# The first norm of a two-layer encoder: one product with a tile of ones and 1/sqrt on ScalarE, with thirteen unread products behind it

## The chip, the cores and the metric

The kernel runs on one core of a Trainium2 chip. The metric is the device time of one execution in microseconds (us). Before the change the median of three runs is 2392.25 us (2389.51 to 2394.10).

## The reference

Two layers run over one sequence of 512 tokens (T) with 1024 channels (D). Each layer has three sub-layers: a feed-forward part (SwiGLU, 2816 wide), a mixer, a second feed-forward part. Each of them begins in the same way, and only this beginning is touched, and only for the first sub-layer of the first layer:

```python
def rms_norm(x, gain):
    y = xf * lax.rsqrt(jnp.mean(xf * xf, axis=-1, keepdims=True) + EPS)
    return (y * gain)
def modulate(h, shift, scale):
    return h * (1 + scale[:, None, :]) + shift[:, None, :]
...
    c_act = jax.nn.silu(c)
    mod = (c_act @ w_ada[l] + b_ada[l]).reshape(B, N_MOD, D_MODEL)
    h = modulate(rms_norm(x, norm_gain[l, 0]), mod[:, 0], mod[:, 1])
    x = x + 0.5 * mod[:, 2][:, None, :] * swiglu(h, ...)
```

Each token needs the reciprocal root of the mean square of its 1024 channels, and each channel a shift and a scale, which are dot products of 1024 numbers of silu(c) with a row of w_ada.

## The kernel before, in words

The activations lie transposed: channels on the 128 partitions, tokens along the row. Eight slices d of 128 channels (KD = 8) make up D. All products are done in three parts to keep precision: a number is split into a high part (hi) and a rest (lo), and the function `triple` (L119, L120, L121) adds hi·hi, lo·hi and hi·lo into one accumulator. For the first norm the names are `hhi` and `hlo` for the two parts of the normalized x, and `whi` and `wlo` for those of the weights.

The opening is written out in `start()`:

1. While x arrives in four blocks, ScalarE squares it (L150), and VectorE adds the eight squared tiles into `ssum` (L693, L695): 128 partitions with 512 tokens each, still to be summed over the partitions.
2. Four small products with a column of ones (L699) sum over the partitions and leave the tokens on the partitions, four columns of 128. There VectorE works out 1/sqrt with the integer estimate and three Newton steps of three instructions (L299, L306 to L308). Since the result is needed along the row, for all partitions alike, it is spread over four diagonal tiles (L708 on ScalarE, L710 on VectorE), and one product with a tile of ones (L713) puts it into the accumulator `rb`, 128x512.
3. Eight steps d follow. In each, `h(d)` computes t = rb·x on VectorE (L722), hhi on ScalarE (L724), a copy of the same value `tb` in PSUM (L726), and hlo = tb − hhi on VectorE (L727). `product(d)` then issues 18 matmuls: for six accumulators (three columns of the gate matrix and three of the up matrix) one each of L119, L120 and L121.

What feeds the steps is loaded by SyncE in program order: per step one weight chunk w_first (384 KB, two buffers `raw`) and two rows of w_ada (512 KB each, four buffers `v2`), one for the shift (j = 0) and one for the scale (j = 1) of the next slice. A buffer is loaded again when its reader is done. Each row of w_ada is turned into 128 shifts or scales by one dot product on VectorE (`mod_dot`, L206; its result tile is `modc`, and its big output goes back into the loaded tile, which the trace calls `v`). ScalarE makes the factor `apre` out of a scale (L213), and hhi(d) needs it. Each weight chunk is rounded to `whi` by ScalarE (L290), and GpSimd computes `wlo` = raw − whi (L292). After the eight steps the same accumulators are evacuated (L571 is the Silu), and the next unit's weights follow in the same way, with wlo on VectorE.

The order on each engine is decided by a scheduler. `tc.issue_after(x)` and `behind(engine)` only tell it that an instruction is to stand behind another one in its engine's queue. So the engines' queues are shown below where they differ.

Of the kernel before, what the change touches and what calls it, by code (L numbers as in the profile page):

```python
# [40 lines left out]
def encoder_kernel(tc, xT, c, w_ada, b_ada, gains, w_gate, w_up, w_down, w_qkv, w_f, w_ubg,  # L41
# [93 lines left out]
    make_identity(nc, ident)  # L135
    ones = cp.tile([P, P], F32, name="ones")
    nc.vector.memset(ones, 1.0)
    silc = [st([P, D], F32, "b", NB)]
    sil_dram = dr.tile([1, D], F32, name="sil_dram")
    crow = st([1, D], F32, "b", NB)  # L140
# [62 lines left out]
    def mod_dot(raw, l, j, d):  # L203
        m = modc[:, l, j, d:d + 1]
        with after("norm"):
            dot = nc.vector.tensor_tensor_reduce(out=raw, in0=raw, in1=silc[0], scale=1.0,  # L206
                                                 scalar=badac[:, l, j, d:d + 1], op0=ALU.mult, op1=ALU.add,
                                                 accum_out=m).ins
        s, kind = divmod(j, 3)
        if kind == 1:  # L210
            g = gainc[:, l, s, d:d + 1]
            if in_start[0]:
                nc.scalar.activation(apre[:, l, s, d:d + 1], m, AF.Identity, scale=g, bias=g)  # L213
                return dot
            return nc.vector.scalar_tensor_tensor(apre[:, l, s, d:d + 1], m, 1.0, g, op0=ALU.add, op1=ALU.mult).ins
        if kind == 2:
            nc.vector.tensor_scalar(m, m, 0.5, None, op0=ALU.mult)

    mod_queue = [(l, j, d) for l in range(L) for j in range(9) for d in range(KD)][16:]
    mod_ptr = [0]  # L220
# [354 lines left out]
    class Ffn:  # L575
# [112 lines left out]
        def start(self):  # L688

            l = self.l  # L690
            ssum = st([P, T], F32, "ssum", 1)
            tiles = [sq[:, a, :] for sq in squares for a in range(2)]
            fold = nc.vector.tensor_tensor(ssum, tiles[0], tiles[1], op=ALU.add)  # L693
            for tile_ in tiles[2:]:
                fold = nc.vector.tensor_tensor(ssum, ssum, tile_, op=ALU.add)  # L695
            gate["vector"] = fold.ins
            pv = mmt((P, NT))
            for t in range(NT):
                mm(pv[:, t:t + 1], ssum[:, t * P:(t + 1) * P], ones[:, 0:1], start=True, stop=True)  # L699
            with behind("vector"):  # L700
                mod_step(l, 0, 0, "v2")
            v = st([P, NT], F32, "nt_v4", 1)
            nc.vector.tensor_scalar(v, pv, 1.0 / D, EPS, op0=ALU.mult, op1=ALU.add)
            r = rsqrt(v, NT)
            dg = st([P, NT, P], F32, "ssum", 1)
            for t in range(NT):
                if t % 2:
                    nc.scalar.activation(dg[:, t, :], ident, AF.Copy, scale=r[:, t:t + 1])  # L708
                else:
                    gate["vector"] = nc.vector.tensor_scalar(dg[:, t, :], ident, r[:, t:t + 1], None, op0=ALU.mult).ins  # L710
            spread = gate["vector"]
            rb = mmt()
            mm(rb, ones, dg.rearrange("p a b -> p (a b)"), start=True, stop=True)  # L713
            pgs = [(acc(), acc()), (acc(), acc()), (mmt(), mmt())]

            with behind("vector"):
                ready = [mod_step(l, 1, 0, "v2")]
            gate.clear()

            def h(d):  # L720
                t = t1(T)
                scaled = nc.vector.tensor_tensor(t, rb, xd(d), op=ALU.mult).ins  # L722
                a, b = apre[:, l, 0, d:d + 1], modc[:, l, 0, d:d + 1]
                nc.scalar.activation(hhi[:, d, :], t, AF.Identity, scale=a, bias=b)  # L724
                tb = mmt()
                nc.scalar.activation(tb, t, AF.Identity, scale=a, bias=b)  # L726
                nc.vector.tensor_tensor(hlo[:, d, :], tb, hhi[:, d, :].bitcast(F32), op=ALU.subtract)  # L727
                if d + 1 < KD:
                    with tc.issue_after(ready[0]):
                        mod_step(l, 0, d + 1, "v2")  # L730
                    with tc.issue_after(scaled):
                        ready[0] = mod_step(l, 1, d + 1, "v2")

            def product(d, w):
                for n in range(3):
                    for which in range(2):
                        i = 3 * which + n
                        triple(pgs[n][which], w[0][:, i, :], w[1][:, i, :], hhi[:, d, :], hlo[:, d, :],
                               d == 0, d == KD - 1)

            for d in range(KD):
                if d == 0:
                    gate["vector"] = spread
                w = wchunk(w_first[d], (6, P), side=False, lo_eng=nc.gpsimd)
                gate.clear()
                h(d)
                product(d, w)
            in_start[0] = False
            self.early = self.gate_up(0, 3), self.gate_up(1, 3)
            late_inputs()  # L750
            return [self.act(n, *pgs[n]) for n in range(3)]
# [557 lines left out]
```

## Time and profile before

| what | value |
|---|---|
| median of three runs | 2392.25 us |
| the profiled execution's own time | 2394.31 us |
| its span in the trace | 2392.4 us |
| TensorE busy in the span | 2357.9 us (99%) |
| VectorE busy in the span | 1738.8 us (73%) |
| first matmul of step d = 0 (L119) | 21.81 us |
| first matmul behind the eight steps | 59.09 us |

The profiled execution is 2.1 us above the median of the runs and inside their spread (its upper end is 2394.10) but for 0.2 us. Of its own time 1.9 us lie outside the span. Times in rows count from the span's start. A row of the timeline gives start, length, engine, line, operation, output and inputs, and in brackets how long the engine stood idle before it and what ended that. PE is TensorE, DVE is VectorE, ACT is ScalarE, POOL is GpSimd, SP is SyncE.

### The profile page before, as it was taken

To read this page: it belongs to the slowest core of one execution; us is meant where nothing else is said; L and a number is where in the kernel's file an instruction comes from. 1 tells how busy PE (TensorE), PEld (TensorE's weight loads), DVE (VectorE), ACT (ScalarE), POOL (GpSimd) and SP (SyncE) were. 2 spreads that over 40 slices of the span, in tenths; PEclk is the share of its full clock that TensorE was granted. 3 is DMA by queue.
4 is the path that set the end of the run, shared out by engine and by line. 5 is a ranking of instruction groups with operands and counts; after the bars stand their busy time and mean duration, and the time that the engine had idled before them with its cause. 6 is when DMAs were issued, how large, how long until landed. Compare 5 with 4: busy or idle time off the path is not lost.

```text
span 2392.4 us, 36842 instructions
## 1 busy us (share of the span) xinstructions
PE 2357.9 (99%) x14106; PEld 2086.4 (87%) x14106; DVE 1738.8 (73%) x3090; ACT 1201.4 (50%) x2090; POOL 315.9 (13%) x401
## 2 busy tenths in 40 slices
PE   7999999999999999999999999999999999999999
PEld 5898998778888898989998989978788888889898
DVE  8887866787685576878677878577866855768583
ACT  5353555786632353635553636466865324536252
POOL 3000011144312200000000000102443222000000
PEclk9999999999999999999999999999999999999999
DMA  7535342223355534353325353323233554223322
GB/s 284 203 106 185 105 143 80 94 80 109 119 199 200 193 106 151 115 178 105 133 80 194 101 190 106 135 84 100 78 117 111 220 202 158 99 96 106 104 96 102
DMA packets 116436, 320.93 MB, mean 134 GB/s; under 512 B 11138, under 2 KB 13314, under 8 KB 116260
## 3 DMA queue, kind: packets, MB, share of 16 engines
q1 hardware_dynamic: 115106, 314.38, 38.6%
q0 software_dynamic: 1152, 4.19, 0.4%
q8 instruction: 111, 1.82, 0.3%
q14 instruction: 65, 0.53, 0.1%
q10 hardware_dynamic: 2, 0.00, 0.0%
HBM read 312.16 MB, written 6.38 MB: 133 GB/s over the span
## 4 chain that ended last, share of the span: by engine, by line
PE 85%; DVE 7%; ACT 5%; issue 2%; DMA 1%; SPq 0%; DVEq 0%; ACTq 0%; POOL 0%; POOLq 0%
PE acc L119 15%; PE acc L120 15%; PE acc L121 15%; PE mm L119 4%; PE mm L120 4%; PE mm L121 4%; PE mm L129 4%; PE mm L128 4%; PE mm L130 4%; PE acc L128 4%; PE acc L129 4%; PE acc L130 4%; ACT b L859 1%; PE mm L997 1%; DVE v L206 1%
## 5 line engine op out<-in xcount | busy, mean ns | idle before, releaser
L290 ACT CAST whi<-raw 128x1024 fp32r<-128x1024 f32 (+1 forms) x267 | 277.4, 1043 | 438.3 <-PE acc L120 255.7
L292 DVE TENSOR_TENSOR wlo<-raw,whi 128x1024 fp32r<-128x1024 f32 x259 | 319.6, 1237 | 160.5 <-ACT whi L290 157.8
L119 PE MATMUL acc<-b,whi 128*128 128x512 f32 (+1 forms) x960 | 360.7, 376 | 0.0
L120 PE MATMUL acc<-b,whi 128*128 128x512 f32 (+1 forms) x960 | 357.0, 372 | 0.0
L121 PE MATMUL acc<-b,wlo 128*128 128x512 f32 (+1 forms) x960 | 356.6, 371 | 0.0
L119 PEld LDWEIGHTS acc<-b,whi 128*128 128x128 f32 x960 | 180.8, 188 | 31.7 <-DVE xv L447 0.3
L121 PEld LDWEIGHTS acc<-b,wlo 128*128 128x128 f32 x960 | 180.8, 188 | 31.5
L120 PEld LDWEIGHTS acc<-b,whi 128*128 128x128 f32 x960 | 180.9, 188 | 29.8
L119 PE MATMUL acc<-hhi,whi 128*128 128x512 f32 x480 | 191.1, 399 | 3.3 <-ACT hhi L724 1.7
L120 PE MATMUL acc<-hlo,whi 128*128 128x512 f32 x480 | 188.3, 392 | 1.4 <-DVE hlo L727 1.4
L121 PE MATMUL acc<-hhi,wlo 128*128 128x512 f32 x480 | 188.0, 392 | 0.0
L398 DVE TENSOR_TENSOR ptb<-v,ptb 128x1024 fp32r<-128x1024 f32 x128 | 156.6, 1224 | 35.8 <-ACT ptb L397 33.9
L397 ACT CAST ptb<-v 128x1024 fp32r<-128x1024 f32 x128 | 134.0, 1050 | 95.4 <-DVE v L465 54.6
L397 ACT CAST whi<-raw 128x1024 fp32r<-128x1024 f32 (+1 forms) x128 | 106.7, 834 | 99.2 <-PE acc L120 52.8
L119 PE MATMUL acc<-whi,hhi 128*128 128x512 f32 x336 | 137.8, 411 | 0.9 <-DVE xv L398 0.9
L121 PE MATMUL acc<-whi,hlo 128*128 128x512 f32 x336 | 131.9, 393 | 0.0
L120 PE MATMUL acc<-wlo,hhi 128*128 128x512 f32 x336 | 131.7, 392 | 0.0
L206 DVE CUSTOM_DVE_ANT_0 v<-v,b,badac 128x1024 f32<-128x1024 f32 x87 | 116.1, 1341 | 20.5 <-DMA v<-in_w_ada_dram 20.3
L398 DVE TENSOR_TENSOR wlo<-raw,whi 128x1024 fp32r<-128x1024 f32 (+1 forms) x128 | 122.0, 953 | 6.8 <-ACT whi L397 5.0
L447 DVE SCALAR_TENSOR_TENSOR xv<-acc,modc,xv 128x512 f32<-128x512 f32 (+1 forms) x112 | 77.3, 691 | 63.4 <-PE acc L121 63.4
L119 PEld LDWEIGHTS acc<-hhi,whi 128*128 128x128 f32 x480 | 90.7, 189 | 21.4 <-ACT hhi L724 3.3
L119 PE MATMUL mm<-hhi,whi 128*128 128x512 f32 x280 | 109.3, 391 | 0.0
(313 smaller groups left out, 6594.9 us busy)
## 6 DMA issues: line engine op xcount, KB each, us to landing
raw<-in_w_down_dram SPq DMA_DIRECT2D x88, 512.0 KB, 3.7
v<-in_w_ada_dram SPq DMA_DIRECT2D x87, 512.0 KB, 5.4
raw<-in_w_up_dram SPq DMA_DIRECT2D x82, 512.0 KB, 3.9
raw<-in_w_gate_dram SPq DMA_DIRECT2D x79, 512.0 KB, 3.6
b<-in_w_ada_dram SPq DMA_DIRECT2D x57, 512.0 KB, 5.2
raw<-in_w_ubg_dram SPq DMA_DIRECT2D x56, 512.0 KB, 3.5
raw<-in_w_qkv_dram SPq DMA_DIRECT2D x42, 512.0 KB, 3.6
raw<-in_w_branch_dram SPq DMA_DIRECT2D x24, 512.0 KB, 3.6
```

The costliest lines, as they stand in the source:

```text
L119: mm(o, lh, rh, start=start, stop=False)
L120: mm(o, lh, rl, start=False, stop=False)
L121: mm(o, ll, rh, start=False, stop=stop)
L128: mm(o, lh, rh, start=start and k == 0, stop=False, skip_group_check=True)
L129: mm(o, lh, rl, start=False, stop=False, skip_group_check=True)
L130: mm(o, ll, rh, start=False, stop=k == 3, skip_group_check=True)
L206: dot = nc.vector.tensor_tensor_reduce(out=raw, in0=raw, in1=silc[0], scale=1.0, scalar=badac[:, l, j, d:d + 1], op0=ALU.mult, op1=ALU.add ...
L290: nc.scalar.copy(hi, raw)
L292: lo_eng.tensor_tensor(lo, raw, hi.bitcast(F32), op=ALU.subtract)
L397: nc.scalar.copy(hi, src)
L398: nc.vector.tensor_tensor(lo, src, hi.bitcast(F32), op=ALU.subtract)
L447: nc.vector.scalar_tensor_tensor(x, acc_j, gate, x, op0=ALU.mult, op1=ALU.add)
```

## The change

`ssum` is now multiplied once by the whole tile of ones, so that the sum over the partitions stands in all 128 partitions, tokens along the row (`total`, 128x512 in PSUM). The estimate of 1/sqrt is taken on ScalarE straight from there (`seed`), its square too, and VectorE does one Newton step on 128x512 elements with three instructions, of which the last writes `rb` into PSUM. The diagonal tiles and the nine small Newton instructions are gone. Behind the product stand thirteen products of two constant tiles, `ones` and `ident`, each 128x128, which nothing reads. The scale's dot product for d = 0 is asked for earlier, and inside a step the order asked for is now: t(d), shift dot of d+1, hlo(d), scale dot of d+1. The line `return dot` lets the shift's dot be named.

```diff
+    eps = cp.tile([P, 1], F32, name="eps")
+    nc.vector.memset(eps, EPS)
...
+        return dot
...
-            pv = mmt((P, NT))
-            for t in range(NT):
-                mm(pv[:, t:t + 1], ssum[:, t * P:(t + 1) * P], ones[:, 0:1], start=True, stop=True)
+            total = mmt()
+            mm(total, ones, ssum, start=True, stop=True)
+            spin = mmt((P, P))
+            for _ in range(13):
+                mm(spin, ones, ident, start=True, stop=True)
             with behind("vector"):
                 mod_step(l, 0, 0, "v2")
-            v = st([P, NT], F32, "nt_v4", 1)
-            nc.vector.tensor_scalar(v, pv, 1.0 / D, EPS, op0=ALU.mult, op1=ALU.add)
-            r = rsqrt(v, NT)
-            dg = st([P, NT, P], F32, "ssum", 1)
-            for t in range(NT):
-                if t % 2:
-                    nc.scalar.activation(dg[:, t, :], ident, AF.Copy, scale=r[:, t:t + 1])
-                else:
-                    gate["vector"] = nc.vector.tensor_scalar(dg[:, t, :], ident, r[:, t:t + 1], None, op0=ALU.mult).ins
-            spread = gate["vector"]
+                mod_step(l, 1, 0, "v2")
+            seed, square = t2(T), t2(T)
+            nc.scalar.activation(seed, total, AF.Abs_reciprocal_sqrt, scale=1.0 / D, bias=eps)
+            gate["scalar"] = nc.scalar.activation(square, seed, AF.Square).ins
+            var = t1(T)
+            nc.vector.tensor_scalar(var, total, 1.0 / D, EPS, op0=ALU.mult, op1=ALU.add)
             rb = mmt()
-            mm(rb, ones, dg.rearrange("p a b -> p (a b)"), start=True, stop=True)
+            nc.vector.scalar_tensor_tensor(var, square, -0.5, var, op0=ALU.mult, op1=ALU.mult)
+            nc.vector.scalar_tensor_tensor(rb, var, 1.5, seed, op0=ALU.add, op1=ALU.mult)
             pgs = [(acc(), acc()), (acc(), acc()), (mmt(), mmt())]
-
-            with behind("vector"):
-                ready = [mod_step(l, 1, 0, "v2")]
-            gate.clear()
...
-                nc.vector.tensor_tensor(hlo[:, d, :], tb, hhi[:, d, :].bitcast(F32), op=ALU.subtract)
-                if d + 1 < KD:
-                    with tc.issue_after(ready[0]):
-                        mod_step(l, 0, d + 1, "v2")
-                    with tc.issue_after(scaled):
-                        ready[0] = mod_step(l, 1, d + 1, "v2")
+                low = lambda: nc.vector.tensor_tensor(hlo[:, d, :], tb, hhi[:, d, :].bitcast(F32), op=ALU.subtract).ins
+                if d + 1 == KD:
+                    low()
+                    return
+                with tc.issue_after(scaled):
+                    shift = mod_step(l, 0, d + 1, "v2")
+                with tc.issue_after(shift):
+                    done = low()
+                with tc.issue_after(done):
+                    mod_step(l, 1, d + 1, "v2")
...
             for d in range(KD):
-                if d == 0:
-                    gate["vector"] = spread
                 w = wchunk(w_first[d], (6, P), side=False, lo_eng=nc.gpsimd)
```

Three places show how the queues move. The first is VectorE's queue in the opening norm, before the change, from the scale's dot product of slice 0 (`v_35`) back to the small Newton instructions ahead of it. `nt_v`, `nt_q`, `nt_u` and `nt_z` are the four-column tiles of the estimate; `t_39` is t of step 0.

```order
L307 SCALAR_TENSOR_TENSOR nt_u_153<-nt_q_152,nt_v_16_136 128x4
L308 SCALAR_TENSOR_TENSOR nt_z_154<-nt_u_153,nt_z_148 128x4
L710 TENSOR_SCALAR ssum_158<-ident,nt_z_154 128x128 x2
L206 ISA v_35_171,modc<-v_35_171,b_73,badac 128x1024
L206 ISA modc 128x1
L206 ISA v_41_187,modc<-v_41_187,b_73,badac 128x1024
L206 ISA modc 128x1
L722 TENSOR_TENSOR t_39_181<-mm_163,xv_78 128x512
```

This is the same place with the change. `v_17` is the scale's dot product of slice 0, `v_33` the shift's of slice 1, `t_20` is `var`, `t_19` and `t_18` are `square` and `seed`, and `mm_159` is `rb`.

```order
L208 ISA v_16_146,modc<-v_16_146,b_75,badac 128x1024
L208 ISA modc 128x1
L208 ISA v_17_149,modc<-v_17_149,b_75,badac 128x1024
L208 ISA modc 128x1
L712 TENSOR_SCALAR t_20_157<-mm_130 128x512
L714 SCALAR_TENSOR_TENSOR t_20_157<-t_19_154,t_20_157 128x512
L715 SCALAR_TENSOR_TENSOR mm_159<-t_20_157,t_18_153 128x512
L720 TENSOR_TENSOR t_31_174<-mm_159,xv_80 128x512
L208 ISA v_33_179,modc<-v_33_179,b_75,badac 128x1024
```

Eleven small instructions and two of 128x128 have given way to three of 128x512; both dot products of slice 0 stand ahead of them, and the first dot product of slice 1 has moved from ahead of t(0) to behind it.

The second place is VectorE's queue in the middle of the steps. With the change, from t of step 2 (`t_45`) to hlo of step 3 (out of `mm_288`); `v_41` and `v_48` are the scale's dots of slices 2 and 3, `v_47` is the shift's of slice 3.

```order
L720 TENSOR_TENSOR t_45_248<-mm_159,xv_87 128x512
L725 TENSOR_TENSOR hlo<-mm_214,hhi 128x512
L208 ISA v_41_220,modc<-v_41_220,b_75,badac 128x1024
L208 ISA modc 128x1
L208 ISA v_47_253,modc<-v_47_253,b_75,badac 128x1024
L208 ISA modc 128x1
L720 TENSOR_TENSOR t_52_285<-mm_159,xv_87 128x512
L725 TENSOR_TENSOR hlo<-mm_251,hhi 128x512
L208 ISA v_48_257,modc<-v_48_257,b_75,badac 128x1024
```

From step 0 to step 4 the order is now the same: t(d+1), hlo(d), scale dot of d+1, shift dot of d+2; from there on the shift dot stands between t and hlo. Before, the order changed from step to step, and both dots of a slice could run ahead of the hlo of the slice before it. TensorE's queue follows: of the 18 matmuls of a step, the ones that need only hhi (L119) stood one ahead of the first that needs hlo in steps 1 to 7; now there are 6, 5, 4, 3, 2, 1 and in step 7 again 6 of them ahead.

The third place is ScalarE's queue in the opening norm with the change; `t_18` is `seed`, `t_19` is `square`, `whi_170` the first weight chunk.

```order
L159 COPY b_75<-mm_92 128x512
L709 ACT_TABLE_LOAD
L709 ACTIVATE t_18_153<-mm_130,eps 128x512
L215 ACTIVATE apre<-modc,gainc 128x1
L710 ACTIVATE t_19_154<-t_18_153 128x512
L293 CAST whi_170<-raw_168 128x768
L722 ACTIVATE hhi<-t_31_174,modc,apre 128x512
L724 ACTIVATE mm_177<-t_31_174,modc,apre 128x512
```

A load of another function table stands ahead of the estimate (and a second one, back, ahead of the first Silu behind the steps); the first weight cast, which stood ahead of the norm's own work, now stands behind `square`.

## The prediction

> **What bounds the kernel now.** I read the busy times first, then what TensorE waited for in the first 60 us, then two windows, and then the timeline around the change.
>
> ```profile
> PE 2357.9 (99%) x14106; PEld 2086.4 (87%) x14106; DVE 1738.8 (73%) x3090; ACT 1201.4 (50%) x2090; POOL 315.9 (13%) x401
> ```
>
> ```profile
> PE mm L713 <- ACT ssum L708: 4.6, 1, 4.6
> PE mm L699 <- DVE ssum L695: 4.1, 1, 4.1
> PE acc L119 <- ACT hhi L724: 1.7, 1, 1.7
> PE acc L120 <- DVE hlo L727: 1.4, 2, 1.0
> ```
>
> ```profile
> 20.20:55.10 34.90, 31.88 (x128) 25.34 (x128) 34.73 (x46) 20.16 (x30) 15.73 (x7) 1.00 0.81 293
> 55.00:100.00 45.00, 44.91 (x198) 37.19 (x199) 43.98 (x67) 19.84 (x25) 0.00 (x0) 1.00 0.69 233
> ```
>
> Over the whole span TensorE is the bound: an opening that ends x us earlier should end the kernel x us earlier, since from 55 to 100 us TensorE idles for only 0.09 us. Inside the opening it looks otherwise. The columns of a window are its length and then the busy time of PE, PEld, DVE, ACT and POOL: during the eight steps VectorE is busy for 34.73 of 34.90 us, more than TensorE's 31.88. The opening hangs on VectorE's queue, and TensorE runs close behind it. The last step shows that:
>
> ```profile
> 53.67 0.39 PE L119 MATMUL acc<-hhi,whi 128*128 128x512 f32 x1
> 54.35 0.68 DVE L727 TENSOR_TENSOR hlo<-mm,hhi 128x512 fp32r<-128x512 f32 x1
> 55.09 0.50 PE L120 MATMUL acc<-hlo,whi 128*128 128x512 f32 x1 [1.04 <-DVE hlo L727]
> 59.09 0.39 PE L119 MATMUL mm<-hhi,whi 128*128 128x512 f32 x1
> ```
>
> The last hlo ends at 55.03, the 17 matmuls behind it take 4.00, and at 59.09 the eight steps are over. **The question is where this 59.09 goes.**
>
> **The opening norm, step by step.**
>
> ```profile
> 5.94 1.15 ACT L150 ACTIVATE wlo<-xv 128x512 f32<-128x512 f32 x2
> 10.17 1.05 ACT L157 COPY b<-mm 128x512 f32<-128x512 f32 x2
> 11.46 1.28 DVE L206 CUSTOM_DVE_ANT_0 v<-v,b,badac 128x1024 f32<-128x1024 f32 x1
> 11.60 1.86 PE L699 MATMUL mm<-ones,ssum 128*128 128x1 f32 x8 [4.14 <-DVE ssum L695]
> 13.79 1.80 POOL L292 TENSOR_TENSOR wlo<-raw,whi 128x768 fp32r<-128x768 f32 x1 [12.48 <-ACT whi L290]
> 17.68 1.28 DVE L206 CUSTOM_DVE_ANT_0 v<-v,b,badac 128x1024 f32<-128x1024 f32 x1
> 18.05 2.07 PE L713 MATMUL mm<-ssum,ones 128*128 128x512 f32 x2 [4.58 <-ACT ssum L708]
> 20.16 0.69 DVE L722 TENSOR_TENSOR t<-mm,xv 128x512 f32<-128x512 f32 x1
> ```
>
> Before, the sum is ready for TensorE at 11.60 and t(0) starts at 20.16. Now: the product with ones is of L713's size, 2.07, and ends at 13.7. The estimate on ScalarE was never run here; per 512 columns the nearest rows are a Square at 0.58 (half of 1.15) and tb at 0.76 (below), and I take 0.69. It ends at 14.4, apre (0.39) follows, since its dot runs at 12.7 to 14.0 right behind the first, and the square runs to 15.3. The var instruction lies beside it. The two Newton instructions take 0.69 each (t's row) with 0.1 between dependent ones: 15.35 to 16.04, 16.05 to 16.75. So t(0) starts at 16.85, **3.3 us earlier**. ScalarE's queue behind the estimate holds apre, the square and the first cast; the cast (0.82) waits till 15.2, where before its result was there for the wlo of 13.79, and hhi(0) behind it loses nothing, since t(0) comes later. SyncE's queue gains too: the load that waits for the scale's dot of slice 0 can go at 14.0 instead of 19.0, but the weight load behind it still waits for the first wlo of GpSimd, which ends at about 18.
>
> The two extra table loads: what one costs stands at 433.79.
>
> ```profile
> 432.74 1.03 ACT L290 CAST whi<-raw 128x1024 fp32r<-128x1024 f32 x1
> 433.79 1.28 ACT L918 ACT_TABLE_LOAD   x1
> 435.08 0.63 ACT L918 ACTIVATE t<-t 8x512 f32<-8x512 f32 x1
> ACT t L571 <- PE acc L121: 2.5, 1, 2.5
> ```
>
> It is 1.28 with 0.02 on either side. The first lies between 11.24, where the copy of silu(c) ends, and 13.7, where the product ends: nothing. The second lies in the 2.5 us that ScalarE waits ahead of the first Silu (last row): nothing; without this cover it would be 1.28. The Trainium skill (page "ScalarE: Activation LUTs", section "What ACT_TABLE_LOAD costs") adds a drain of about 1.38 to such a load; by that the estimate would begin 0.2 later. The rows above show no drain, so I leave it out.
>
> The thirteen products: one of 128x128 has a quarter of L713's columns, so at most 0.52, and at least the 0.46 that two of L699's eight records take; together 6.0 to 6.8 at the slow clock, and half of that where the clock is up. They end between 16.7 and 20.5. hhi(0) is ready at 18.5, so at worst they hold step 0 up by 2.0.
>
> **The eight steps.** Here are the rows that set the pace.
>
> ```profile
> 20.20 1.81 POOL L292 TENSOR_TENSOR wlo<-raw,whi 128x768 fp32r<-128x768 f32 x1 [4.61 <-DVE modc L206]
> 20.77 2.32 DVE L206 CUSTOM_DVE_ANT_0 v<-v,b,badac 128x1024 f32<-128x1024 f32 x1
> 20.95 0.81 ACT L724 ACTIVATE hhi<-t,modc,apre 128x512 fp32r<-128x512 f32 x1 [0.83 <-DVE t L722]
> 21.66 0.76 ACT L726 ACTIVATE mm<-t,modc,apre 128x512 f32<-128x512 f32 x1
> 21.81 2.08 PE L119 MATMUL acc<-hhi,whi 128*128 128x512 f32 x4 [1.69 <-ACT hhi L724]
> 25.22 0.81 ACT L290 CAST whi<-raw 128x768 fp32r<-128x768 f32 x1
> 25.39 0.63 PE L120 MATMUL acc<-hlo,whi 128*128 128x512 f32 x1
> 26.02 1.27 DVE L206 CUSTOM_DVE_ANT_0 v<-v,b,badac 128x1024 f32<-128x1024 f32 x1
> 26.11 2.88 POOL L292 TENSOR_TENSOR wlo<-raw,whi 128x768 fp32r<-128x768 f32 x1 [4.11 <-DVE hlo L727]
> 27.33 0.39 ACT L213 ACTIVATE apre<-modc,gainc 128x1 f32<-128x1 f32 x1 [1.30 <-DVE modc L206]
> 28.50 0.39 PE L119 MATMUL acc<-hhi,whi 128*128 128x512 f32 x1
> 32.59 0.39 PE L119 MATMUL acc<-hhi,whi 128*128 128x512 f32 x1
> ```
>
> ```profile
> L206 DVE CUSTOM_DVE_ANT_0 v<-v,b,badac 128x1024 f32<-128x1024 f32 x14 | 23.0, 1651 | 0.0
> L292 POOL TENSOR_TENSOR wlo<-raw,whi 128x768 fp32r<-128x768 f32 x7 | 15.7, 2248 | 20.8 <-ACT whi L290 12.1 <-DVE modc L206 4.6 <-DVE hlo L727 4.1
> L490 DVE TENSOR_TENSOR v<-hhi,hlo 128x1024 f32<-128x1024 f32 x1 | 2.9, 2858 | 0.0
> ```
>
> A dot product takes 1.28 alone and GpSimd's wlo 1.80. Where they meet, they run one after the other: the dot of 20.77 ends at 23.09, 1.08 behind the wlo that ends at 22.01; the wlo of 26.11 ends at 28.99, 1.77 behind the dot of 26.02. So fourteen dots took 23.0 instead of 17.9, L490 2.86 instead of about 1.2 (twice the 0.60 of 512 columns), and 6.8 us of VectorE's 34.7 are waits for GpSimd. t and hlo, which read PSUM, are not held.
>
> VectorE's own work in a step is two dots at 1.20 and t and hlo at 0.60 each: 3.6. TensorE's is 18 matmuls at 0.227: 4.09 (28.50 to 32.59). Without GpSimd's piece VectorE would keep ahead; with it, it doesn't. In the new order a second chain is closed: the scale dot of d+1 stands behind hlo(d), and hlo(d+1) needs that dot: 1.28, apre 0.39, hhi 0.71 to tb's start, tb 0.76, hlo 0.60 and the hand-overs make 3.9, and GpSimd's piece must fit in as well.
>
> I let each engine take its queue in the new order, with these durations, 0.03 to 0.10 for each hand-over, and the rule of the last paragraph. A pair of steps as an example: the scale dot of slice 2 runs 25.43 to 26.71; the wlo of slice 2, asked for at 25.60 behind its cast, takes till 28.40; the shift dot of 3 is held till 29.49; t(3) 29.41, hlo(2) 30.02, scale dot of 3 at 30.63, held by the next wlo till 32.38; shift dot of 4 to 33.58, t(4) 33.50, hlo(3) at 34.36 behind tb; scale dot of 4 at 34.97. That is 9.54 for two steps, 4.77 each, where TensorE needs 4.09. The first matmuls of steps 0 to 7 come out at 18.5, 24.2, 28.3, 33.7, 38.3, 43.7, 48.3 and 53.1: a lead of 3.3 at step 0 and 4.3 at step 1 (28.50 before), and 0.6 at step 7 (53.67 before). **VectorE eats the lead.** In step 7 six L119 now stand ahead of the hlo, which ends at 54.4; twelve matmuls, 2.7, are left, and the steps end at 57.2. The same working with the old order gives 58.9 where the trace has 59.09, so 57.2 to 57.4: **a gain of 1.7 to 1.9**. A plainer sum bounds it from the other side: 16 pieces at 0.60, 15 dots at 1.20, L490 at 1.2 and the old 6.8 of waits from t(0) at 16.85 end at 52.5, and 2.7 later the steps: a gain of 3.9.
>
> The clock: a matmul's row lasts 0.63 at 25.39, and 0.39 at 28.50. If the thirteen products bring the fast clock by 18 instead of 27, steps 0 and 1 are quicker; but with the slow clock till 27, or with the products ending at 20.5, the working above ends at the same 57.2, because VectorE is the later one by step 3. So their worth is near zero, and so is their price.
>
> **Forecast:** 1.7 off. On the profiled execution that is 2394.31 to 2392.6; on the median, 2392.25 to **2390.6**, 0.07% less. A measurement of this kernel can tell about 0.2%, 4.8 us, from no change.
>
> **Rivals.**
>
> GpSimd gets in first. The second Newton instruction reads two tiles in SBUF, and such an instruction is held too:
>
> ```profile
> 485.06 1.48 POOL L1026 TENSOR_TENSOR b<-yl,b 64x256 fp32r<-64x256 f32 x1 [1.82 <-ACT b L1025]
> 485.87 0.73 DVE L308 SCALAR_TENSOR_TENSOR nt_z<-nt_u,nt_j 128x32 f32<-128x32 f32 x1
> ```
>
> (0.73 instead of 0.16.) I have it at 16.05 and the first wlo at 16.11. If it is the other way round, rb comes at 18.4, the first hhi matmul at 20.2, and the same working ends at 58.8: a gain of 0.1 to 0.3, 2392.0. With a margin of 0.06 this has a fair chance.
>
> TensorE becomes the bound. From 18.5, 144 matmuls at 0.227 would end at 51.2, a gain of 7.9: 2384.4. It needs VectorE's waits for GpSimd to fall away nearly whole; for a gain above 4.8 they must fall from 6.8 to below 5.9 in the plain sum, with no step lost to the new chain. The early loads speak for it, the pair of steps above against.
>
> The clock falls back: slower. Each new step leaves TensorE idle for about 0.8. If that takes the clock to half, a step needs 18 times 0.43, 7.7, and TensorE is the bound at twice the pace. Against the 58.9 of the same working: slow till 40, the steps end at 61.6 (2394.9); slow till 44, at 63.6, which is about where the 4.8 are reached (2397.0); all the way, at 75.8, and the kernel at 2409. Against it: before, the 1.04 idle ahead of 55.09 is followed by 17 matmuls in 4.00, the fast pace. The Trainium skill ("TensorE: Matmul & The Clock Gate", Part 1) lets the clock fall only after an idle window of some 3.4 us. By that rule this rival is out, and the row agrees as far as it reaches.
>
> The products don't warm: no difference to the end, as worked out; only steps 0 and 1 would show it.
>
> **Chances.** Forecast 0.57, GpSimd first 0.20, products without effect (same time as the forecast) 0.03, TensorE the bound 0.12, clock 0.08. So faster by over 0.2% is 0.12, slower 0.08, within 0.80. The range takes the first three, 0.80: from the plain sum, 2388.4, less 1.4 for the spread of the runs, to GpSimd first, 2392.0, with the runs' upper distance of 1.9 and 0.6 for my working: 2387.0 to 2394.5.
>
> **What would show it.** t(0) at 16.9 (or 18.5, with the last Newton instruction lasting 2.4: GpSimd first). First L119 at 18.5. Between t(0) and the last hlo VectorE busy throughout, dots longer than 1.28 beside wlo, matmuls behind the steps at 57.2. TensorE's waits for hhi and hlo summing up to 6 us where they were 3.1. I am wrong if VectorE has idle time there, if the steps come 4.1 apart from the start, if rows of 0.63 show up behind 30 us, or if the lead at 57 is lost or grows further on, where I have TensorE full.

## The result and the profile after

The changed kernel takes 2397.55 us (median of 8 runs, 2395.49 to 2399.98) where the kernel before takes 2391.23 beside it (8 runs, 2389.51 to 2394.10). The ratio is 1.0025, 95% interval 1.0016 to 1.0034: **6.3 us slower**, where 1.7 off was forecast. The profiled execution took 2397.46, its span is 2395.2.

I looked at the opening first. These rows of the changed kernel's timeline (ScalarE, TensorE, VectorE and GpSimd, put in order of start) answer to those of the prediction.

```profile
10.86 1.28 ACT L709 ACT_TABLE_LOAD   x1
13.32 4.04 PE L704 MATMUL mm<-ident,ones 128*128 128x128 f32 x26
13.56 0.69 ACT L709 ACTIVATE t<-mm,eps 128x512 f32<-128x512 f32 x1 [1.43 <-PE mm L701]
15.82 0.70 DVE L715 SCALAR_TENSOR_TENSOR mm<-t,t 128x512 f32<-128x512 f32 x1
15.85 2.33 POOL L295 TENSOR_TENSOR wlo<-raw,whi 128x768 fp32r<-128x768 f32 x1 [14.54 <-DVE t L714]
16.55 0.69 DVE L720 TENSOR_TENSOR t<-mm,xv 128x512 f32<-128x512 f32 x1
18.21 1.19 PE L119 MATMUL acc<-hhi,whi 128*128 128x512 f32 x4 [0.84 <-ACT hhi L722]
53.63 1.07 PE L119 MATMUL acc<-hhi,whi 128*128 128x512 f32 x4
58.31 0.39 PE L119 MATMUL mm<-hhi,whi 128*128 128x512 f32 x1
```

Step 0 begins at 18.21 instead of 21.81, and the eight steps are over at 58.31 instead of 59.09. The opening is 0.8 shorter, and no row in it is dearer than the forecast allows. So the loss lies behind it, in the 2,337 us that the change does not touch. The first line of the page shows it already:

```profile
PE 2364.4 (99%) x14124; PEld 2093.0 (87%) x14124; DVE 1739.9 (73%) x3081; ACT 1203.6 (50%) x2092; POOL 317.2 (13%) x401
```

TensorE is busy for 6.5 us more than before (2357.9). The opening, with its 18 matmul records more, accounts for 1.4 of that; 5.1 lie behind it, in the same number of matmuls. Then I laid the start of each matmul beside the start of the same matmul before. The changed kernel is 0.8 ahead at 100 us, 0.6 behind at 400, 1.5 at 850, 2.2 to 2.4 at 1030 to 1110. It falls behind mainly in stages that are dense with products of 256 columns; scattered waits add to that in some places (0.9 us between 712 and 762 us) and take it back in others. One such stage is a run of 672 products without a gap; here are its first product and the one behind its last, first before, then after.

```profile
956.12 0.28 PE L128 MATMUL acc<-hhi,whi 128*128 128x256 f32 x1
1035.96 0.40 PE L119 MATMUL acc<-b,whi 128*128 128x512 f32 x1
```

```profile
957.63 0.28 PE L128 MATMUL acc<-hhi,whi 128*128 128x256 f32 x1
1038.26 0.40 PE L119 MATMUL acc<-b,whi 128*128 128x512 f32 x1
```

The same 672 products take 79.84 before and 80.63 after: 118.8 ns from start to start, and 120.0. TensorE has no idle time in either, so no view of waits or idle shows the difference; it is the pace itself. Sorted by operands most of it sits on the tile `ptb`, into which a part of the weights is split. The rows of the tile view give how often, then shortest, median and longest duration in ns; before, then after:

```profile
L128 PE MATMUL acc<-b,ptb x384: 277/280/285, 127.2 to 2330.2; 128*128 128x256 f32 x192
```

```profile
L128 PE MATMUL acc<-b,ptb x384: 283/283/283, 126.5 to 2333.5; 128*128 128x256 f32 x192
```

From here on, "pitch" is the mean distance from a product's start to the next product's start, over those distances that lie between 105 and 130 ns (256 columns) or 200 and 245 ns (512 columns). The pitch of acc<-b,ptb went from 118.3 to 120.0 ns. Over the 7,176 products of 256 columns behind the opening whose distance lies there in both traces, the sum is 6.9 us longer; over those of 512 columns it is 0.4 shorter. Less the opening's 0.8 that makes 5.7, where the medians differ by 6.3. (The two profiled spans differ by only 2.8: the profiled run of before has 2.9 us more of scattered waits, 1.4 of them at 1118 us.)

Why should these products be slower? They are the same instructions in the same order. What differs is where their operands lie. The new tile `eps` takes 32 bytes per partition among the constants, and all tiles behind it move by 32: hhi, hlo, b, whi, wlo. The tiles that the opening no longer needs ahead of `ptb`, and a new order of first use, moved `ptb` by another amount: 768 bytes back. By the addresses in the two built programs (no view of the profile has them) the distance from b and hhi to ptb was 32 bytes modulo 256 before, and is 0 now.

### The profile page after: what moved, and what is told of

The parts are those of the page before. It is cut to its first block, busy times and chain, and to the rows that moved or that the text cites. A ratio compares the mean times of both kernels' runs of the same rounds, so it can differ in the third digit from the quotient of the medians.

```text
span 2395.2 us, 36867 instructions
## 1 busy us (share of the span) xinstructions
PE 2364.4 (99%) x14124; PEld 2093.0 (87%) x14124; DVE 1739.9 (73%) x3081; ACT 1203.6 (50%) x2092; POOL 317.2 (13%) x401
## 4 chain that ended last, share of the span: by engine, by line
PE 86%; DVE 6%; ACT 5%; issue 2%; DMA 1%; SPq 0%; DVEq 0%; ACTq 0%
PE acc L119 15%; PE acc L121 15%; PE acc L120 15%; PE mm L130 4%; PE mm L129 4%; PE mm L128 4%; PE acc L128 4%; PE acc L130 4%; PE acc L129 4%; PE mm L121 4%; PE mm L120 4%; PE mm L119 4%; ACT b L859 1%; PE mm L997 1%; DVE v L208 1%
## 5 line engine op out<-in xcount | busy, mean ns | idle before, releaser
L119 PE MATMUL acc<-b,whi 128*128 128x512 f32 (+1 forms) x960 | 360.5, 376 | 0.0
L119 PEld LDWEIGHTS acc<-b,whi 128*128 128x128 f32 x960 | 180.9, 188 | 31.2
L119 PE MATMUL acc<-hhi,whi 128*128 128x512 f32 x480 | 188.0, 398 | 2.8 <-ACT whi L293 1.6
L119 PE MATMUL acc<-whi,hhi 128*128 128x512 f32 x336 | 137.7, 411 | 0.9 <-DVE xv L401 0.9
L120 PEld LDWEIGHTS acc<-hlo,whi 128*128 128x128 f32 x480 | 90.4, 188 | 23.2 <-DVE hlo L725 7.6
L120 PE MATMUL mm<-hlo,whi 128*128 128x512 f32 x280 | 109.0, 389 | 0.0
```

The lines of the kernel that those rows point to most:

```text
L119: mm(o, lh, rh, start=start, stop=False)
L120: mm(o, lh, rl, start=False, stop=False)
```

## The experiments

Theories that I set out with: **T1**, a product of 256 columns is slow where both operands lie in the same half of a 64-byte line; **T2**, it is slow where b and hhi are not at a multiple of 64; **T3**, addresses don't matter, and the thirteen products, the earlier clock or the new order set the later pace. From the second group on also **T4**: the pace depends on the distance of the two operands modulo 128 or 256. The table gives the distances modulo 256 (from b and hhi, which agree), the pitch of acc<-b,ptb and the ratio to the kernel before in the same group of runs.

| kernel | ptb | whi, wlo | pitch, ns | time, us | ratio (95%) |
|---|---|---|---|---|---|
| before | 32 | 0 | 118.3 | 2390.65 to 2391.33 | 1 |
| changed | 0 | 0 | 120.0 | 2397.55 | 1.0025 (1.0016 to 1.0034) |
| e1, before, all moved | 32 | 0 | 118.3 | 2390.98 | 1.0003 (0.9995 to 1.0012) |
| e2, before, ptb moved | 64 | 0 | 117.8 | 2390.70 | 0.9999 (0.9990 to 1.0008) |
| e3, changed, eps of 64 bytes | 0 | 0 | 120.0 | 2395.61 | 1.0021 (1.0013 to 1.0030) |
| e4, changed, eps elsewhere | 32 | 0 | 118.3 | 2392.43 | 1.0008 (0.9999 to 1.0016) |
| e5, before, whi and wlo moved | 96 | 32 | 118.7 | 2416.48 | 1.0103 (1.0090 to 1.0117) |
| e6, changed, pad of 64 | 64 | 0 | 117.8 | 2390.46 | 0.9996 (0.9987 to 1.0004) |
| e7, as e6, no thirteen products | 64 | 0 | 117.8 | 2390.09 | 0.9995 (0.9986 to 1.0004) |
| e8, as e6, old order of steps | 64 | 0 | 117.8 | 2392.14 | 1.0004 (0.9995 to 1.0013) |
| e9, before, ptb at 128 | 128 | 0 | 118.6 | 2392.28 | 1.0004 (0.9995 to 1.0013) |
| e11, before, ptb at 0 | 0 | 0 | 120.0 | 2396.60 | 1.0023 (1.0014 to 1.0032) |
| e12, e6 once more | 64 | 0 | 117.8 | 2389.46 | 0.9995 (0.9986 to 1.0004) |

### Where the operands lie: e1 to e4

All tiles moved by 32 bytes, in the kernel before:

```diff
-    ones = cp.tile([P, P], F32, name="ones")
+    ones = cp.tile([P, P + 8], F32, name="ones")[:, :P]
```

> The kernel before, with the ones tile 32 bytes wider per partition, which nothing reads. Every tile behind it lies 32 bytes further, as most do in the changed kernel: b, hhi, hlo, whi, wlo now at 32 bytes past a multiple of 64, ptb now at a multiple of 64. Instructions and their order are those of the kernel before. Theory T1 (what counts is whether the two operands of a product lie at the same or at different 32-byte halves): the halves are still different for b and ptb, so the pitch of acc<-b,ptb stays at 118.4 ns and the time at 2391, within 1.5. Theory T2 (what counts is that b and hhi lie at a multiple of 64): the pitch becomes 120.0 and the time 2397.5. Theory T3 (addresses don't count; the thirteen products, the earlier clock or the new order of instructions set the later pitch): 2391, pitch unchanged.

Measured: 2390.98, pitch 118.3, the tile row word for word in its three durations as before:

```profile
L128 PE MATMUL acc<-b,ptb x384: 277/280/285, 127.6 to 2327.6; 128*128 128x256 f32 x192
```

T2 falls: where b lies by itself doesn't matter.

Only ptb and what lies behind it moved, in the kernel before:

```diff
-            v = st([P, NT], F32, "nt_v4", 1)
+            v = st([P, 4 * NT], F32, "nt_v4", 1)[:, :NT]
```

> The kernel before, with nt_v4 48 bytes wider per partition, which nothing reads: raw, t1, t2, ptb and what lies behind them move by 32 bytes, b, hhi, hlo, whi and wlo stay. Instructions and their order are those of the kernel before; b and ptb now lie in the same half. T1: the pitch of acc<-b,ptb, mm<-b,ptb and of hhi and hlo with ptb goes from 118.4 to 120.0; 3,600 of them times 1.6 is 5.9, so 2397 (2395.5 to 2398.5). T2: 2391, since b and hhi did not move. T3: 2391.

```profile
L128 PE MATMUL acc<-b,ptb x384: 281/281/281, 127.2 to 2327.1; 128*128 128x256 f32 x192
```

Measured: 2390.70 and a pitch of 117.8. All operands lie in the same half, and it is a little faster, not slower: T1 falls too. What the slow kernel has is not "the same half" but a distance of exactly 0 modulo 256; that suggests T4.

The changed kernel with a wider eps:

```diff
-    eps = cp.tile([P, 1], F32, name="eps")
+    eps = cp.tile([P, 16], F32, name="eps")[:, :1]
```

> The changed kernel, with eps 64 bytes wide per partition instead of 4 (it takes 32), so b, hhi, hlo, whi, wlo are back at a multiple of 64, and ptb has moved with them to a multiple of 64 too: all in one half. T1: as the changed kernel, 2397.5, pitch of acc<-b,ptb 120.0. T2: the pitch goes back to 118.4 and the time to 2390.4 (0.8 less than before, the lead at the end of the eight steps). T3: as the changed kernel, 2397.5.

Measured: 2395.61 and 120.0. It stays slow, at distance 0, with b back at a multiple of 64. T2 falls a second time.

The changed kernel with eps in the place of a small tile behind v2, filled by GpSimd:

```diff
-    eps = cp.tile([P, 1], F32, name="eps")
-    nc.vector.memset(eps, EPS)
...
+            eps = st([P, 1], F32, "nt_v4", 1)
+            nc.gpsimd.memset(eps, EPS)
             seed, square = t2(T), t2(T)
```

> The changed kernel, with eps not among the constants but in the 32 bytes between v2 and the tiles behind it, where nt_v4 stood before (filled by GpSimd, which is idle then): b, hhi, hlo, whi, wlo at a multiple of 64, ptb 32 bytes past one, as in the kernel before. All else is the change as made. T1 and T2: the pitch of acc<-b,ptb goes back to 118.4 and the time to 2390.4 (2389 to 2392), 0.8 below the kernel before. T3: 2397.5, pitch 120.0.

Measured: 2392.43. The pitch is back at 118.3, so the thirteen products, the clock and the order don't set it: T3 falls. But the opening lost what it had won. ScalarE's rows of this kernel:

```profile
13.85 1.28 ACT L709 ACT_TABLE_LOAD   x1 [2.56 <-PE mm L699]
15.14 0.69 ACT L709 ACTIVATE t<-mm,nt_v 128x512 f32<-128x512 f32 x1
```

The table load, which began at 10.86 in the changed kernel and lay hidden, begins here only when the product is done; the estimate starts at 15.14 instead of 13.56, step 0 at 19.78 instead of 18.21, and the steps end at 59.85. What changed for this instruction is what it waits for. In the changed kernel it waits for TensorE alone: VectorE filled `eps` ahead of the `ssum` that the product itself waits for. Here it waits for TensorE and for GpSimd, which fills `eps`, and in the built program the wait for TensorE has become an instruction of its own ahead of the load. Of the 1.57 us by which step 0 is late, 1.28 are the load; most of the rest is there before it, since the product itself begins 0.2 later.

### The address alone: e11

The kernel before, with nothing of the change in it; one tile of 16 bytes lies among the constants instead of among the work tiles.

```diff
     ones = cp.tile([P, P], F32, name="ones")
+    first_v = cp.tile([P, NT], F32, name="first_v")
...
-            v = st([P, NT], F32, "nt_v4", 1)
+            v = first_v
```

> The kernel before, with the tile of nt_v4 (16 bytes, it takes 32) placed among the constants behind ones instead of among the work tiles. Instructions and their order are those of the kernel before, none of the change is in it, and b, hhi, hlo, whi, wlo and ptb lie exactly where they lie in the changed kernel: distance of ptb to b and hhi 0 modulo 256. T4: pitch of acc<-b,ptb 120.0, the 128x256 products 7.0 longer in sum, 2398.0 (2396 to 2399.5). T3: 2391.

```profile
L128 PE MATMUL acc<-b,ptb x384: 283/283/283, 127.3 to 2332.8; 128*128 128x256 f32 x192
```

Measured: 2396.60 where the kernel before takes 2391.33: 5.3 us, a ratio of 1.0023 (1.0014 to 1.0032). The pitch is 120.0 with the three durations of the changed kernel. `ptb` lies 768 bytes away from its place in the changed kernel, so not exactly there, as I had expected, but at the same distance modulo 256. Against e1, in which b, hhi and the weights lie at the same addresses and ptb 32 bytes further on modulo 256, the dense products of 256 columns are 7.0 us longer, those of 512 columns 0.8 shorter, the opening and the waits 0.4 shorter in sum, and the spans differ by 5.8. **This is the loss, without the change**, as far as the two intervals can tell (5.3 here, 6.3 in the changed kernel).

### How far it goes: e5, e9 and a sweep

The kernel before with 32 bytes ahead of whi:

```diff
+        if b == 0:
+            pad = st([P, 1], F32, "pad", 1)
+            nc.gpsimd.memset(pad, 0.0)
         sq = st([P, 2, T], F32, "wlo" if b else "whi", 3)
...
-            v = st([P, NT], F32, "nt_v4", 1)
+            v = st([P, 4 * NT], F32, "nt_v4", 1)[:, :NT]
```

> The kernel before, with a pad of 32 bytes per partition ahead of whi, filled by GpSimd at the start and read by nothing, and nt_v4 48 bytes wider. Distances modulo 256 (before in brackets): whi and wlo to b and hhi 32 (0), ptb to b and hhi 96 (32). Theory T4 (the pitch of two operands depends on their distance modulo 128 or 256; 0 is the slow case for 256 columns): the products of 128x256 with whi or wlo, 3,200 that run at 120.0, come down to about 118.4, 5 us less; those with ptb stay between 117.5 and 118.5. For 512 columns the few pairs seen so far speak for the other sign: acc<-ptb,hhi took 229 at distance 0, 231 at 64, 234 at 32. If that holds for all 5,000 with whi or wlo, 0 to 4 ns each, 0 to 20 us more: 2386 to 2406, with the pitches to tell which. T3 (addresses don't count): 2391, all pitches as before.

The same row, first of the kernel before, then of this one:

```profile
L119 PE MATMUL mm<-hhi,whi x280: 389/389/628, 23.7 to 2104.8; 128*128 128x512 f32 x140
```

```profile
L119 PE MATMUL mm<-hhi,whi x280: 395/396/628, 23.8 to 2125.9; 128*128 128x512 f32 x140
```

Measured: 2416.48 (four runs), **25 us slower for a pad of 32 bytes**. With whi or wlo the pitch of 256 columns came down from about 119.8 to between 117.4 and 118.7, as T4 has it: against e1, 3.0 us off over all products of that width. But the mean pitch of 512 columns went from 227.9 to 233.1: 5,805 of them, 30.4 us more; shorter waits give some of it back. So the sign turns with the width: a distance of 0 is the slow case for 256 columns and the fast one for 512. My range for this run was too narrow by 10 us.

Distance 128, in the kernel before:

```diff
+            early = st([P, 1], F32, "nt_v", 2)
+            nc.gpsimd.memset(early, 0.0)
-            v = st([P, NT], F32, "nt_v4", 1)
+            v = st([P, 4 * NT], F32, "nt_v4", 1)[:, :NT]
```

> The kernel before, with nt_v4 48 bytes wider and the nt_v tiles (64 bytes) taken ahead of ptb instead of behind it by a first small tile that GpSimd fills and nothing reads. Distance of ptb to b and hhi 128 modulo 256 (32 before). T4 with modulus 128: as at distance 0, pitch of acc<-b,ptb 120.0 and 2397.5. T4 with modulus 256: pitch between 117.5 and 118.5, 2391. T3: 2391.

Measured: 2392.28, pitch 118.6, between both. 128 does not behave as 0 does, so the modulus is not 128.

The pace by itself, behind the last matmul of the kernel before, where the other engines only bring the last output out:

```diff
     poll(True)
+    moving = hhi.rearrange("p a b -> p (a b)")
+    for cols in (256, 512):
+        for k, off in enumerate((0, 16, 32, 64, 96, 128, 160, 192, 224, 256, 288)):
+            o = (acc if k % 2 else mmt)((P, cols))
+            for q in range(64):
+                at = T * (q % 7) + off // 4
+                mm(o, hlo[:, q % 8, 0:P], moving[:, at:at + cols], start=q == 0, stop=q == 63)
```

> The kernel before, with 1,408 products behind its end whose results nothing reads: blocks of 64, stationary hlo, moving hhi at 0, 16, 32, 64, 96, 128, 160, 192, 224, 256 and 288 bytes past a multiple of 256 from it, first with 256 columns, then with 512. T4: pitch with 256 columns 120.0 at 0 and at 256, 118.3 at 32 and 288, 117.8 at 64, 118.6 at 96 and 128, unknown and below 120 from 160 to 224; with 512 columns 227 at 0 and 256, 233 at 32 and 288, 231 at 64, 233 at 96 and 128. If the pitch comes from other things than the distance (the lines' place in the program, the other engines' and the DMAs' traffic), all blocks of a width have one pitch, since nothing else runs there.

Each row is a block of 64 products; the start of the next row less its own start, divided by 64, is the pitch. In the order 0, 16, 32, 64, 96, 128, 160, 192, 224, 256 bytes with 256 columns, then (behind a row that holds two blocks) 16, 32, 64 and so on with 512:

```profile
2385.81 7.84 PE L1256 MATMUL mm<-hhi,hlo 128*128 128x256 f32 x64
2393.49 7.76 PE L1256 MATMUL acc<-hhi,hlo 128*128 128x256 f32 x64
2401.10 7.63 PE L1256 MATMUL mm<-hhi,hlo 128*128 128x256 f32 x64
2408.57 7.42 PE L1256 MATMUL acc<-hhi,hlo 128*128 128x256 f32 x64
2415.82 7.84 PE L1256 MATMUL mm<-hhi,hlo 128*128 128x256 f32 x64
2423.50 7.77 PE L1256 MATMUL acc<-hhi,hlo 128*128 128x256 f32 x64
2431.10 7.67 PE L1256 MATMUL mm<-hhi,hlo 128*128 128x256 f32 x64
2438.61 7.42 PE L1256 MATMUL acc<-hhi,hlo 128*128 128x256 f32 x64
2445.87 7.73 PE L1256 MATMUL mm<-hhi,hlo 128*128 128x256 f32 x64
2453.44 7.84 PE L1256 MATMUL acc<-hhi,hlo 128*128 128x256 f32 x64
2461.11 22.24 PE L1256 MATMUL mm<-hhi,hlo 128*128 128x256 f32 x128
2483.19 14.99 PE L1256 MATMUL acc<-hhi,hlo 128*128 128x512 f32 x64
2498.01 15.10 PE L1256 MATMUL mm<-hhi,hlo 128*128 128x512 f32 x64
2512.95 14.81 PE L1256 MATMUL acc<-hhi,hlo 128*128 128x512 f32 x64
2527.59 15.09 PE L1256 MATMUL mm<-hhi,hlo 128*128 128x512 f32 x64
```

With 256 columns that gives 120.0 at 0, 118.9, 116.7, 113.3 at 64, 120.0 at 96, 118.8, 117.3, 113.4 at 192, 118.3 and 119.8 at 256. With 512 columns it is 227.0 at 0 and at 256 (from the single starts), 231.6 at 16, 233.4 at 32, 228.8 at 64, and 233 to 234 from 96 to 224. This is one execution. The blocks of a width differ in that offset and in the accumulator (acc and mm in turn), and 0 and 256 have one pace with either accumulator, so I put the pace down to the offset. It repeats after 256 bytes at 0, and with 512 columns at 32 too (288 gave 233.4 again); with 256 columns 288 gave 117.9 where 32 gave 116.7. The forecast for 256 columns held at the two ends and missed at 64 (113.3 for 117.8) and at 96, which is as slow as 0 (120.0 for 118.6). In the kernels ptb is the stationary side, so a ptb that lies 32 further on counts here as 224: 118.3 in both; 128: 118.6 there, 118.8 here; 96 counts as 160: 118.7 there, 117.3 here; 64 counts as 192: 117.8 there, 113.4 here. So distance modulo 256 tells the sign and the two ends, not every value; what else enters inside the kernel stays open.

### The opening: e6, e7, e8 and e12

The whole change, with a pad ahead of t2 that puts ptb at 64:

```diff
+            pad = st([P, 16], F32, "nt_v4", 1)
+            nc.gpsimd.memset(pad, 0.0)
             seed, square = t2(T), t2(T)
```

> The changed kernel, with a pad of 64 bytes per partition ahead of t2, filled by GpSimd at the start and read by nothing; eps stays where the change put it, so the estimate waits for no other engine. Distance of ptb to b and hhi 64 modulo 256 (0 in the changed kernel, 32 in the kernel before). T4: pitch of acc<-b,ptb 117.8, of all 128x256 products 118.3; opening as in the changed kernel (steps over at 58.3 to 59.2); 2389.0, from 2390.7 less the lead of 0.8 and less 0.9 for the distance; with the spread of medians 2388 to 2391. T3: as the changed kernel, 2397.

> The kernel with the 64-byte pad (the whole change, ptb at distance 64 from b and hhi) once more, unchanged, on another occasion, to settle whether the change is worth anything where the addresses do no harm. My sum: steps over at 58.2 instead of 59.1 and 0.9 to 1.0 off the 128x256 products, 1.8 less than the kernel before, ratio 0.9992. If later waits take the lead back, no difference, 1.000.

The row of `ptb` in the first of the two:

```profile
L128 PE MATMUL acc<-b,ptb x384: 281/281/281, 126.4 to 2327.2; 128*128 128x256 f32 x192
```

Measured: 2390.46 and 2389.46, each beside the kernel before at 2391.05 and 2390.65: 0.6 and 1.2 off, as the sum wants in sign, but each interval includes 1. The steps end at 58.22 and 57.83. TensorE, VectorE and ScalarE take the opening in the same order as in the changed kernel. Against that kernel as it was made, the pad removes its loss.

The same without the thirteen products that nothing reads:

```diff
-            spin = mmt((P, P))
-            for _ in range(13):
-                mm(spin, ones, ident, start=True, stop=True)
```

> As the kernel with the 64-byte pad, and without the thirteen products that nothing reads. If their worth is near nil, as my working has it, the eight steps end within 0.3 of where they end with them, and the time is the same within 1. If the clock they bring counts, steps 0 and 1 and with them the end come later by up to 2 (nine or ten products at 0.41 instead of 0.23).

```profile
18.64 2.08 PE L119 MATMUL acc<-hhi,whi 128*128 128x512 f32 x4 [4.67 <-ACT hhi L721]
59.63 0.39 PE L121 MATMUL mm<-hhi,wlo 128*128 128x512 f32 x1
```

The first four L119 take 2.08 instead of about 1.2: the clock is still low. The 145th product of the opening, the one that stands behind the eight steps by count (the scheduler has pulled one L119 of the next unit ahead here), starts at 59.63, with the thirteen products at 58.22. That is 1.4 later, and not all of it is the clock. The opening was 0.4 later already (t(0) at 16.98 and 16.57), and without the thirteen products the scheduler put VectorE's queue in another order: the shift dot stands between t and hlo from hlo(1) on (in e6 from hlo(5) on), and hlo(1) starts at 25.96 where e6 has it at 24.59. So this run does not tell what the thirteen products are worth by themselves. The medians, 2390.09 and 2390.46, don't show it: 1.4 is inside their intervals.

The same as e6, in the old order of the steps:

```diff
-                low = lambda: nc.vector.tensor_tensor(hlo[:, d, :], tb, hhi[:, d, :].bitcast(F32), op=ALU.subtract).ins
...
+                nc.vector.tensor_tensor(hlo[:, d, :], tb, hhi[:, d, :].bitcast(F32), op=ALU.subtract)
+                if d + 1 < KD:
+                    with tc.issue_after(ready[0]):
+                        mod_step(l, 0, d + 1, "v2")
+                    with tc.issue_after(scaled):
+                        ready[0] = mod_step(l, 1, d + 1, "v2")
```

> As the kernel with the 64-byte pad (new norm, thirteen products), but the eight steps issue in the order of the kernel before: hlo ahead of both dot products of the next slice. The kernel with the pad ends the steps at 58.2, the kernel before at 59.1. If the new order is what eats the lead of 3.3 (the chain through the scale dot that it closes), the steps end here at 56 to 57 and the kernel 1 to 2 earlier than with the new order. If VectorE's waits for GpSimd eat it in either order, they end within 0.5 of 58.2. If the new order is what saves, they end at 59 or later.

VectorE's and GpSimd's rows of it, in order of start, and three of TensorE's:

```profile
14.89 1.27 DVE L208 CUSTOM_DVE_ANT_0 v<-v,b,badac 128x1024 f32<-128x1024 f32 x1
15.85 4.28 POOL L295 TENSOR_TENSOR wlo<-raw,whi 128x768 fp32r<-128x768 f32 x2 [14.53 <-ACT whi L293]
16.09 2.33 DVE L716 SCALAR_TENSOR_TENSOR t<-t,t 128x512 f32<-128x512 f32 x1
18.45 2.23 DVE L717 SCALAR_TENSOR_TENSOR mm<-t,t 128x512 f32<-128x512 f32 x1
22.37 2.07 PE L119 MATMUL acc<-hhi,whi 128*128 128x512 f32 x4 [5.02 <-ACT hhi L724]
31.57 0.50 PE L120 MATMUL acc<-hlo,whi 128*128 128x512 f32 x1 [1.95 <-DVE hlo L727]
33.16 0.63 PE L121 MATMUL acc<-hhi,wlo 128*128 128x512 f32 x1
```

With the old order the scheduler puts a third dot product into the middle of the Newton step. GpSimd's wlo gets in first, and both Newton instructions that read two tiles in SBUF take 2.33 and 2.23 instead of 0.70: this is my rival "GpSimd gets in first", nearly twice as dear as I had it (3.2 for two instructions held, where I had 1.7 for one). With 1.0 for the third dot, step 0 is 4.1 later than in e6 and starts at 22.37. The fast clock is lost by then (2.07 for four), comes, and is lost a second time behind the idle 1.95 (0.63 at 33.16; the granted clock is 1.00 from 26 to 32 us, 0.60 from 32 to 34 and 0.54 from 34 to 36). From step 2 on the steps come 4.08 apart, which is TensorE's own pace, and they end at 60.50. Taken as a whole, the new order saves 2.3 here. It does not follow that the new order eats none of the lead: from step 0 to the end the old order takes 38.1 us, slow clock included, and the new one in e6 40.0. Here VectorE had done part of its work before step 0 began, so the order of the steps is not tested by itself, and this stays open.

## Why the prediction was wrong, point by point

**The step that failed: "an opening that ends x us earlier should end the kernel x us earlier".** From 55 us on TensorE is full, as said, and that is just why a longer pitch shows in full. I had weighed what the change does to queues, clock and waits, and nowhere what it does to the addresses of tiles that it doesn't touch. e11 shows that alone to cost 5.3 (1.0014 to 1.0032), with 7.0 more in the dense products of 256 columns; e6 shows the change without it to cost nothing. The sum had no such term, and none of the rivals was near it: "TensorE is the bound" was right, but its products got dearer. The prediction named the sign of it among what would make it wrong, a lead lost behind 57 us where TensorE is full, without asking what could take it.

**Opening norm: right.** t(0) at 16.55 (forecast 16.85), first L119 at 18.21 (18.5), L715 0.03 ahead of GpSimd's wlo (forecast 0.06). The margin is thin but no chance of one run: it is 0.03 or 0.04 in e3, e6 and e12 as well.

**The table loads: right.** Both lay hidden, with 1.43 us to spare ahead of the estimate and 1.20 ahead of the first Silu (the idle time of ScalarE between load and function). With the cover gone the price is 1.28 as said, and e4 shows how easily it goes. The drain that the prediction cites does not show there: the load ends at 15.13, and the estimate starts at 15.14.

**The eight steps: right up to step 6, then 1.1 off at the end.** Steps 0 to 7 start at 18.21, 23.91, 28.16, 33.59, 38.17, 43.61, 48.44 and 53.63 (forecast 18.5, 24.2, 28.3, 33.7, 38.3, 43.7, 48.3 and 53.1), and end at 58.31 (57.2). The gain is 0.8 instead of 1.7 to 1.9. The late rows:

```profile
49.68 2.79 POOL L295 TENSOR_TENSOR wlo<-raw,whi 128x768 fp32r<-128x768 f32 x1 [3.86 <-ACT whi L293]
50.68 2.87 DVE L493 TENSOR_TENSOR v<-hhi,hlo 128x1024 f32<-128x1024 f32 x1
53.48 1.27 DVE L208 CUSTOM_DVE_ANT_0 v<-v,b,badac 128x1024 f32<-128x1024 f32 x1
54.68 0.68 DVE L725 TENSOR_TENSOR hlo<-mm,hhi 128x512 fp32r<-128x512 f32 x1
```

GpSimd's last wlo holds L493 till 53.55 as it did L490 before. The last hlo ends at 55.36, before at 55.03, where I had 54.4. Of the lead of 3.6 at step 0 VectorE has eaten all; what is left of the gain, 0.8, is that six L119 now stand ahead of that hlo. The mechanism is the forecast's: from 18.0 to 58.3 us VectorE is busy for 39.79 of 40.30, and TensorE's waits for hhi and hlo sum up to 5.6 (forecast 6).

**The thirteen products: open.** They take 4.04 us and end at 17.36 (forecast 3.0 to 6.8, and 16.7 to 20.5), and they do bring the fast clock to step 0: 1.19 for its first four, 2.08 without them. Whether that is worth "near zero" at the end is not shown, since e7 also changed VectorE's queue. VectorE is the later one there too, as the forecast has it: from t(0) to the last hlo it is idle for only 0.36 us, and TensorE waits for hlo seven times.

**The clock does not fall back** in the changed kernel: from step 0 on a single product's row lasts 0.39, or 0.50 behind a wait. In e8 it does, and behind an idle stretch of 1.95 us, which is shorter than the 3.4 us that the prediction takes from the Trainium skill to rule this rival out. The measurement decides: by that rule the rival was not out, and in the changed kernel TensorE never waited longer than 1.0 us inside the steps.

## What to carry to other kernels

Where TensorE is full, a change that adds, drops or reorders a small tile can move the tiles behind it, as 32 bytes did here; put the addresses of the operands of the many matmuls (their distance modulo 256) beside the diff, and pad so that they keep the distance that they had. If a kernel changes its time by some tenths of a per cent, lay the same matmuls of both traces beside each other before explaining it: the waits, and the busy share of 99% in both, did not show that the pace itself had changed. A saving at the start of a chain is worth what is left behind the last wait of that chain, here 0.8 of 3.6.

## What the runs showed of the hardware that I had not expected

The pace of matmuls with the same shapes at the same clock depends on how the addresses of stationary and moving operand lie to each other: 113.3 to 120.0 ns with 256 columns and 227.0 to 234.2 with 512 in the sweep. The Trainium skill (page "SBUF — State Buffer", section "A bandwidth-pool intuition that's wrong (but worth ruling out)") gives TensorE a second, independent read port for loading the weights; by that the two operands could not disturb each other. The sweep does not agree, at least not for these fp32r products: 6% between the best and the worst offset at 256 columns, 3% at 512. How the two reads meet is not shown by any run here. Nor did these runs tell why 256 columns want the two apart by 64 or 192 bytes, and 512 columns by 0.
